# Rope scores as two packed fp32r products, and moved cast orders, in a two-layer conformer/attention trunk

## The chip, the cores and the metric

One core of one Trainium2 chip runs the whole program. The metric is the device time of one execution in microseconds, as the median of several runs.

## The reference

Two layers on 256 tokens of width 1024, all in float32. Each layer is half an FFN, a mixer, half an FFN; a last RMS norm closes the trunk. Layer 0 mixes by a convolution module, layer 1 by latent attention with 8 heads. What the change touches is the FFN and the attention scores:

```python
def swiglu_ffn(h, w1, w3, w2):
    return (jax.nn.silu(h @ w1) * (h @ w3)) @ w2      # 1024 -> 2816 -> 1024

for blk in range(seq // Q_BLOCK):                     # two query blocks of 128
    q0, q1 = blk * Q_BLOCK, (blk + 1) * Q_BLOCK
    s = (jnp.einsum("bqhd,bkhd->bhqk", q_nope[:, q0:q1], k_nope[:, :q1])
         + jnp.einsum("bqhr,bkr->bhqk", q_rope[:, q0:q1], k_rope[:, :q1])) * scale
    s = jnp.where(mask, s, -jnp.inf)                  # chunks of 64 tokens, causal
    p = jax.nn.softmax(s, axis=-1)
    outs.append(jnp.einsum("bhqk,bkhd->bqhd", p, v[:, :q1]))
```

The first query block sees 128 keys and the second 256. The nope part has 128 dimensions per head, the rope part 64, and the rope key is shared by all heads.

## The kernel before

**Products.** A float32 product is mostly done as three products in fp32r, a format with a shorter mantissa: each operand is split into a high part (a cast) and a low part (the value minus its high part), and `mm3` adds low times high, high times high and high times low. Its three matmuls are L332, L335 and L336. Weights come from memory in blocks of 128x2048 floats (`raw`); ScalarE (ACT) casts a block to `hi` in two pieces of 1024 columns and VectorE (DVE) subtracts to get `lo` (`load`, L246 and L247; `load_seven`, L214 and L200). SyncE (SP) issues all these transfers from one queue. Four raw buffers and five hi/lo buffers rotate, so a block is fetched as soon as an older one has been cast.

**FFN.** The 2816 columns go in chunks: five of 512 (c = 0 to 4) and one of 256 (c = 5). In FFNs 1, 2 and 3 (the second of layer 0 and both of layer 1) chunk 3 is done by seven block products in place of eight (`seven_products`): DVE first adds and subtracts blocks of the weights (L200, `raw<-raw,raw`), and between the products DVE adds finished parts to others (`u<-u,p`, line L258 by way of the helper `urgent`). After a chunk, ACT applies silu, DVE multiplies by the other half (`s<-s,u`) and turns 32x32 blocks (L478), two transfers through memory finish the transpose (`gd`, then `gb`, or `rows` for chunks 0 and 1), and ACT and DVE split the result into `Gh` and `Gl` (both L853). Such a pair of split instructions is a gate cast here, and they are listed in `gates`, two per chunk (NT is 2, one per block of 128 tokens).

**Attention.** KN and QN hold the nope keys and queries by head as float32; KR and QR hold the rope ones, also as float32. Heads are paired: rope rows of even heads stand in partitions 0 to 63 and of odd heads in 64 to 127, and the other half of the 128 rows is zero but for two rows that carry the mask (-1e30 times 1). `scores(hd)` runs for each query block one float32 product of KN and QN (L1584) and one of KR and QR (L1585) into one bank; `softmax` follows on DVE and ACT; `probs` transposes the probabilities on TensorE (PE) and ACT copies them (L1612); `values` multiplies with VV (L1621, L1622), and `evicted` splits the result into `Oh` (ACT, L1616) and `Ol` (DVE, L1617). The output projection runs between the heads, on blocks of two heads (`o<-lo,Oh` and so on). Three heads are scored ahead of the second half of the query projection (`nope`), the others after it.

**Order.** The order on each engine is fixed when the program is built: a list scheduler places instructions by priority (`urgent` lifts it), and `order(a, b)` forces a behind b. In `seven_products` such calls hold the gate casts of the chunk just before, and in `mla_in` a loop holds the casts of the first two output blocks behind certain steps of the softmax.

Of the kernel before, what the change touches and what calls it, by code (L numbers as in the profile page):

```python
# [11 lines left out]
F32 = mybir.dt.float32  # L12
# [7 lines left out]
P = 128  # L20
# [69 lines left out]
def trunk(ctx: ExitStack, tc: tile.TileContext, x, xt, first, pos, invf, gfin, wdw,  # L90
# [14 lines left out]
    def uid(s):  # L105
        n_uid[0] += 1
        return f"{s}_{n_uid[0]}"
# [54 lines left out]


    casts = {}

    turns = []
    last_read = [None]
# [21 lines left out]
    def load_seven(j, four, b, pieces):  # L189
        hi = wp.tile([P, HB], F32R, tag="hi", name=uid("hi"))  # L190
        lo = wp.tile([P, HB], F32R, tag="lo", name=uid("lo"))
        n = len(loaded)
        if j == 0:
            b[11], b[12] = fetched(four[0]), fetched(four[1])
        elif j == 1:
            b[22] = fetched(four[3])
        elif j == 2:
            b[21] = fetched(four[2])
        def sub(out, left, right):
            ins = nc.vector.tensor_sub(out, left, right)  # L200
            behind(ins)
            return ins

        if j == 1:
            sub(b[11], b[12], b[11])
            sub(b[12], b[22], b[12])
        elif j == 2:
            sub(b[11], b[22], b[11])
        elif j == 6:
            sub(b[11], b[21], b[11])  # L210
        raw = b[(11, 11, 11, 21, 12, 22, 11)[j]]
        for i in range(pieces):
            c = slice(i * HB // pieces, (i + 1) * HB // pieces)
            casts[n, i] = nc.scalar.copy(hi[:, c], raw[:, c]), sub(lo[:, c], raw[:, c], hi[:, c].bitcast(F32))  # L214
            behind(casts[n, i][0])
        return hi, lo
# [151 lines left out]
    def seven_products(xh, xl, forms, banks, late={}):  # L368


        def rows(a, tb):
            k = slice(4 * a, 4 * a + 4)
            return xh[:, k, tbs(tb)], xl[:, k, tbs(tb)]

        def product(a, b, fresh):
            load_ahead(W_BUFS - 1)
            (hi, lo), = weights(1, False)
            for k in range(4):
                c = slice(k * 512, k * 512 + 512)
                before[:] = [mm3(b, a[0][:, k], a[1][:, k], hi[:, c], lo[:, c], fresh and k == 0, k == 3, before, True)]  # L380

        n0 = n_used[0]
        before = []
        c11, c21, c12, c22 = banks[0, 0], banks[1, 0], banks[0, 1], banks[1, 1]
        product(rows(0, 0), c11, True)
        first = urgent(nc.scalar.copy)(c21, c11)
        for cast in late.values():
            order(cast, first.ins)
        product(forms[0], c22, True)
        kept = tmp.tile([P, 512], F32, tag="s", name=uid("p5"))  # L390
        last = urgent(nc.scalar.copy)(kept, c22)
        product(forms[1], c21, False)
        add = urgent(nc.vector.tensor_add)(c12, c21, kept)
        order(casts[n0 + 5, 0][1], add.ins)
        for high, low in gates[-NT:] if not late else ():
            order(high, last.ins)
            order(low, add.ins)
        low_gates = [low for high, low in gates[-NT:] if not late]
        product(rows(1, 0), c11, False)
        product(forms[2], c21, False)  # L400
        add = urgent(nc.vector.tensor_add)(c22, c21, kept)
        order(casts[n0 + 6, 0][1], add.ins)
        for low in low_gates[1:]:
            order(low, casts[n0 + 6, PIECES - 1][1].ins)
        product(forms[3], c12, False)
        product(rows(1, 1), c21, False)
# [8 lines left out]
    def tbs(tb):  # L415
        return slice(tb * P, (tb + 1) * P)
# [986 lines left out]
    def rope(pool, dst, src, n, cc, sn, tb, after=()):  # L1403

        w = n * 64
        t1, t2 = (pool.tile([P, w], F32, tag=f"rp{w}", name=uid("rp"), bufs=3 if n > 1 else 4) for _ in range(2))
        a = t1[:, :w].rearrange("p (n i f) -> p n i f", i=2, f=32)
        b = t2[:, :w].rearrange("p (n i f) -> p n i f", i=2, f=32)
        full = [P, n, 2, 32]
        turned = [nc.vector.tensor_tensor(a, src, cc[:, tb, :, :].unsqueeze(1).to_broadcast(full), op=ALU.mult)]  # L1410
        for i in range(2):
            turned.append(nc.vector.tensor_tensor(b[:, :, i, :], src[:, :, 1 - i, :],
                                                  sn[:, tb, i, :].unsqueeze(1).to_broadcast([P, n, 32]), op=ALU.mult))
        for ins in turned:
            for first in after:
                order(ins, first.ins)
        nc.vector.tensor_add(dst, t1[:, :w], t2[:, :w])
# [6 lines left out]
    def mla_in(act, X, make_next, cc, sn):  # L1424
# [4 lines left out]
        CKl = act.tile([P, 2, S], F32R, tag="CKl", name="CKl")  # L1429


        KR = act.tile([P, 2, S], F32, tag="KR", name="KR")
        QR = act.tile([P, 2, H // 2, S], F32, tag="QR", name="QR")
        for x, fill in ((KR, -1e30), (QR, 1.0)):
            nc.gpsimd.memset(x, 0.0)
            for parity in range(2):
                for tb in range(NT):
                    row = 64 * (1 - parity) + 32 * tb
                    t = tb * P + (CHUNK if x is KR else 0)
                    nc.gpsimd.memset(x[row:row + 1, parity, ..., t:t + CHUNK], fill)  # L1440

        last_low = [None]

# [108 lines left out]
        last = nope(part, QN, 4, CQh, CQl, 512, 0, (0, 4), turned)  # L1552
        for t in range(NT):
            b = transposed(kd[t], 0, 1, (last,))
            for i in range(2):
                half = slice(64 * i, 64 * i + 64)
                nc.scalar.copy(KR[half, i, tbs(t)], b[half, :P])
        for tb in range(NT):
            b = transposed(qr[tb], 0, 4, (last,)).rearrange("p (j t) -> p j t", t=P)
            for parity, copy in ((0, nc.scalar.copy), (1, nc.vector.tensor_copy)):  # L1560
                half = slice(64 * parity, 64 * parity + 64)
                urgent(copy)(QR[half, parity, :, tbs(tb)], b[half])
        kpart, = weights()
        nope(kpart, KN, 2, CKh, CKl, D, 0, (0, H))
        (hi, lo), = weights()
        for tb in range(NT):
            for d in range(2):
                b = bank("A", "v")
                for k in range(2):
                    c = slice(k * D + d * 512, k * D + d * 512 + 512)  # L1570
                    mm3(b, CKh[:, k, tbs(tb)], CKl[:, k, tbs(tb)], hi[:, c], lo[:, c], k == 0, k == 1)
                kept = nc.scalar.copy(VV[:, tb, d * 512:(d + 1) * 512], b)

        Oh = act.tile([P, H, S], F32R, tag="Oh", name="Oh")
        Ol = act.tile([P, H, S], F32R, tag="CQ", name="Ol")

        score_last, maxima, powers, scaled = [], [], [], []

        def scores(hd):
            b = bank("B", "sc")  # L1580
            sc = {0: b[:, :P], 1: b[:, P:P + S]}
            for qb in range(NT):
                n = (qb + 1) * P
                nc.tensor.matmul(sc[qb], QN[:, hd, tbs(qb)], KN[:, hd, :n], start=True, stop=False)  # L1584
                last = nc.tensor.matmul(sc[qb], QR[:, hd % 2, hd // 2, tbs(qb)], KR[:, hd % 2, :n], start=False,  # L1585
                                        stop=True)
            score_last.append(last)
            return softmax(sc)

# [19 lines left out]
        def probs(pr):  # L1609
            b = transposed(pr, 0, 3)  # L1610
            pt = act.tile([P, 3 * P], F32, tag="ptT", name=uid("ptT"), bufs=2)
            nc.scalar.copy(pt, b[:, :3 * P])  # L1612
            return pt

        def evicted(hd, b):
# [3 lines left out]
        def values(hd, pt):  # L1619
            b = bank("C", "pv")  # L1620
            nc.tensor.matmul(b[:, :S], VV[:, 0, hd * VH:(hd + 1) * VH], pt[:, :S], start=True, stop=False)  # L1621
            nc.tensor.matmul(b[:, P:S], VV[:, 1, hd * VH:(hd + 1) * VH], pt[:, S:], start=False, stop=True)  # L1622

            (urgent if hd in (3, 4, 5, 6) else lambda f: f)(evicted)(hd, b)

        pr, pt = {}, {}
        part, = weights(1, False)
# [1 line left out]

        table = urgent(nc.scalar.activation)(small.tile([P, 1], F32, tag="silu", name="exp"), neghalf, AF.Exp)  # L1630
        order(table, kept.ins)
        pr[0] = scores(0)
        pr[1] = scores(1)
        pr[2] = scores(2)

        for j, i, highs, lows in ((0, 0, None, maxima[2]), (0, 1, None, scaled[0]), (1, 0, powers[2], scaled[1]),
                                  (1, 1, powers[2], scaled[2])):
            for cast, first in zip(casts[n_used[0] + j, i], (highs, lows)):
                if first is not None:
                    order(cast, first.ins)  # L1640
        nope(part, QN, 4, CQh, CQl, 512, 4, (0, 4), score_last[-1:])
        o = Rows(Oh, Ol, H)
        for i in range(2, H + 3):
# [5 lines left out]
                load_ahead(i - 1 + (i == 4))  # L1649
            if i - 2 < H:  # L1650
                pt[i - 2] = probs(pr[i - 2])
            if i - 3 in pt:
                values(i - 3, pt[i - 3])
            if i in (6, 8):
# [164 lines left out]
```

## Time and profile before

| | |
|---|---|
| time, median of 3 runs | 897.49 us (896.9 to 898.99) |
| the profiled execution | 896.07 us, its span 894.3 us |
| PE busy | 886.9 us, 99% of the span |
| DVE busy | 743.1 us (83%) |
| ACT busy | 571.8 us (64%) |
| transfers | 198.94 MB, mean 222 GB/s |
| granted TensorE clock | 0.999 |

The span is what the profile sees from the first to the last instruction; 1.8 us lie around it. A record of a matmul has a modelled end, so its length is more than the time until the next one may start; the time that a matmul costs is read from the starts of those that follow each other. A float32 matmul leaves two records, one in fp32r leaves one.

### The profile page before, as it was taken

How to read it: one execution, taken by the hardware profiler on the slowest of the kernel's cores; microseconds unless marked ns; L12 is line 12 of the kernel's file. 1: busy time of each engine (PE TensorE's matmuls, PEld its weight loads, DVE VectorE, ACT ScalarE, POOL GpSimd, SP SyncE). 2: the span in 40 equal slices, each digit the busy share in tenths (PEclk: the TensorE clock that was granted, in tenths of full speed). 3: DMA queues.
4: the chain of work that ended last, by engine and by line, in shares of the span. 5: the costliest groups of instructions: out<-in, count | busy, mean ns of one | idle time of the engine just before them, and what ended most of it. 6: DMA issues, size and time to landing. Idle time of an engine off the chain costs nothing.

```text
span 894.3 us, 12241 instructions
## 1 busy us (share of the span) xinstructions
PE 886.9 (99%) x4221; PEld 745.9 (83%) x4221; DVE 743.1 (83%) x1083; ACT 571.8 (64%) x993; POOL 104.2 (12%) x227
## 2 busy tenths in 40 slices
PE   9999999999999999999999999999999999999997
PEld 7888888898988888888888888888899888888886
DVE  6787789579998999999588989995768579989973
ACT  7966458488886646667375566673677566474752
POOL 1000000069962000000010000001400010000000
PEclk9999999999999999999999999999999999999999
DMA  9987629834215864939759369495635349378541
GB/s 330 375 303 274 232 59 355 295 121 172 106 60 194 289 258 144 374 109 388 259 175 339 118 218 357 123 392 182 223 142 189 141 154 342 104 260 317 180 196 48
DMA packets 71055, 198.94 MB, mean 222 GB/s; under 512 B 12369, under 2 KB 41937, under 8 KB 51665
## 3 DMA queue, kind: packets, MB, share of 16 engines
q1 hardware_dynamic: 70560, 197.47, 61.8%
q8 instruction: 33, 0.54, 0.2%
q10 hardware_dynamic: 432, 0.69, 0.2%
q14 instruction: 30, 0.24, 0.1%
HBM read 181.87 MB, written 16.25 MB: 222 GB/s over the span
## 4 chain that ended last, share of the span: by engine, by line
PE 92%; DVE 4%; ACT 2%; DMA 1%; issue 0%; SPq 0%; POOL 0%; DVEq 0%; ACTq 0%
PE u L336 16%; PE u L335 16%; PE u L332 16%; PE o L335 9%; PE o L336 9%; PE o L332 9%; PE gate L1005 2%; PE u L411 2%; DVE acc L1094 2%; PE u L1005 2%; PE tp L446 1%; PE a L335 1%; PE a L332 1%; PE a L336 1%; PE nope L336 1%; PE nope L332 1%
## 5 line engine op out<-in xcount | busy, mean ns | idle before, releaser
L247 DVE TENSOR_TENSOR lo<-raw,hi 128x1024 fp32r<-128x1024 f32 (+1 forms) x236 | 276.2, 1212 | 38.8 <-ACT hi L246 37.6
L246 ACT CAST hi<-raw 128x1024 fp32r<-128x1024 f32 (+1 forms) x238 | 236.8, 1044 | 89.3 <-DMA raw<-in_f2w 30.8
L332 PE MATMUL u<-lo,Xh 128*128 128x512 f32 x612 | 238.4, 389 | 0.1
L336 PE MATMUL u<-hi,Xl 128*128 128x512 f32 x612 | 238.3, 389 | 0.0
L335 PE MATMUL u<-hi,Xh 128*128 128x512 f32 x612 | 238.1, 389 | 0.0
L332 PEld LDWEIGHTS u<-lo,Xh 128*128 128x128 f32 x612 | 114.9, 188 | 24.5 <-ACT Xh L598 0.5
L336 PEld LDWEIGHTS u<-hi,Xl 128*128 128x128 f32 x612 | 114.9, 188 | 24.3 <-DVE Xl L465 0.5
L335 PEld LDWEIGHTS u<-hi,Xh 128*128 128x128 f32 x612 | 114.9, 188 | 23.8
L214 ACT CAST hi<-raw 128x1024 fp32r<-128x1024 f32 x98 | 97.7, 1050 | 51.8 <-DVE raw L200 44.9
L200 DVE TENSOR_TENSOR lo<-raw,hi 128x1024 fp32r<-128x1024 f32 x98 | 115.6, 1216 | 7.1 <-ACT hi L214 7.1
L332 PE MATMUL o<-lo,Gh 128*128 128x512 f32 (+1 forms) x276 | 106.6, 386 | 0.0
L335 PE MATMUL o<-hi,Gh 128*128 128x512 f32 (+1 forms) x276 | 106.5, 386 | 0.0
L336 PE MATMUL o<-hi,Gl 128*128 128x512 f32 (+1 forms) x276 | 106.5, 386 | 0.0
L437 POOL TENSOR_TENSOR ms<-ss 128x1 f32<-128x1 f32 x16 | 8.1, 510 | 597.6 <-ACT junk L429 597.6
L200 DVE TENSOR_TENSOR raw<-raw,raw 128x2048 f32<-128x2048 f32 x28 | 63.9, 2283 | 1.8 <-DMA raw<-in_f2w 0.9
L332 PEld LDWEIGHTS o<-lo,Gh 128*128 128x128 f32 x276 | 51.8, 188 | 10.5
L335 PEld LDWEIGHTS o<-hi,Gh 128*128 128x128 f32 x276 | 51.9, 188 | 10.5
L336 PEld LDWEIGHTS o<-hi,Gl 128*128 128x128 f32 x276 | 51.8, 188 | 10.4
L1094 DVE SCALAR_TENSOR_TENSOR acc<-V,dw,acc 128x128 f32<-128x128 f32 (+1 forms) x174 | 53.9, 391 | 0.0
L1115 ACT ACTIVATE prod<-V,dw 128x128 f32<-128x128 f32 (+1 forms) x128 | 45.6, 415 | 1.8 <-POOL Y L1116 1.0
L956 ACT ACTIVATE s<-u,R 128x512 f32<-128x512 f32 (+1 forms) x48 | 30.9, 647 | 24.8 <-PE u L336 24.1
L797 DVE SCALAR_TENSOR_TENSOR h<-o,rh,h 128x512 f32<-128x512 f32 (+1 forms) x18 | 12.9, 719 | 29.2 <-PE o L336 29.2
(265 smaller groups left out, 1257.7 us busy)
## 6 DMA issues: line engine op xcount, KB each, us to landing
raw<-in_f2w SPq DMA_DIRECT2D x66, 1024.0 KB, 6.2
raw<-in_f1w SPq DMA_DIRECT2D x62, 1024.0 KB, 6.5
raw<-in_cw SPq DMA_DIRECT2D x12, 1024.0 KB, 5.5
gd<-gt SPq DMA_DIRECT2D x160, 64.0 KB, 3.0
gb<-gd SPq DMA_DIRECT2D x24, 256.0 KB, 2.8
rows<-gd SPq DMA_DIRECT2D x16, 256.0 KB, 4.4
raw<-in_wo SPq DMA_DIRECT2D x4, 1024.0 KB, 4.9
hd<-rows SPq DMA_DIRECT2D x56, 64.0 KB, 2.4
```

The costliest lines, as they stand in the source:

```text
L200: ins = nc.vector.tensor_sub(out, left, right)
L214: casts[n, i] = nc.scalar.copy(hi[:, c], raw[:, c]), sub(lo[:, c], raw[:, c], hi[:, c].bitcast(F32))
L246: casts[len(loaded), i] = (nc.scalar.copy(hi[:, c], raw[:, c]), low.tensor_sub(lo[:, c], raw[:, c], hi[:, c].bitcast(F32)))
L247: low.tensor_sub(lo[:, c], raw[:, c], hi[:, c].bitcast(F32)))
L332: mm = nc.tensor.matmul(o, ah, bl, start=start, stop=False, skip_group_check=seeded)
L335: nc.tensor.matmul(o, ah, bh, start=False, stop=False, skip_group_check=seeded)
L336: return nc.tensor.matmul(o, al, bh, start=False, stop=stop, skip_group_check=seeded)
L411: mm = nc.tensor.matmul(o, al if kind == "x" else ah, bl if kind == "l" else bh, start=start and n == 0, stop=stop and n == len(kinds) - 1)
L956: nc.scalar.activation(s[:, :w], u[0, tb][:, :w], AF.Silu, scale=X.r[tb])
L1005: mm = nc.tensor.matmul(u[:, t], w[:, c], X.x[:, k, t], start=(k == 0), stop=(k == KT - 1))
L1094: dve_last.append(nc.vector.scalar_tensor_tensor(out if j == j1 - 1 else y, v, w, y, op0=ALU.mult, op1=ALU.add))
L1115: prods_last.append(nc.scalar.activation(p, v, AF.Copy, scale=w))
```

## The change

Three parts.

1. The rope part of the scores. The rope keys are split into a high part KA, held in both halves of the rows, and a low part in KR; the rope queries into a high part in QR and, in a new tile QA, the low part in the half that QR leaves to zeros and the mask, with a copy of the high part in the other half. Then QA times KA gives high times high plus low times high in one product of 128 rows, and QR times KR gives high times low and the mask in another. Both are fp32r. So a query block takes one float32 and two fp32r matmuls in place of two float32 ones. The splits change the copies: two ACT copies for KA and four DVE subtractions for KR in place of four ACT copies; four ACT copies of QR, four DVE subtractions and four DVE copies for QA in place of two ACT and two DVE copies. The second transpose of the queries stands ahead of more of the value products than before.
2. The casts of the first two output blocks: the high ones of the second block now wait for the copies of the first two transposed probabilities, not for the third head's exponentials; the first block's high casts are held by nothing, as before. `evicted` of head 2 is lifted too.
3. In `seven_products`, the low gate casts of the chunk before the last are held behind the third weight difference (`thirds`), and those of the last chunk are held behind casts of the products' last two weight blocks (the high ones) and behind the low cast of the very last (the low ones).

```diff
@@ load_seven
         elif j == 2:
-            sub(b[11], b[22], b[11])
+            thirds[n] = sub(b[11], b[22], b[11])
@@ seven_products
-        last = urgent(nc.scalar.copy)(kept, c22)
+        urgent(nc.scalar.copy)(kept, c22)
...
-        for high, low in gates[-NT:] if not late else ():
-            order(high, last.ins)
-            order(low, add.ins)
-        low_gates = [low for high, low in gates[-NT:] if not late]
+        for high, low in gates[-2 * NT:-NT] if not late else ():
+            order(low, thirds[n0 + 2].ins)
+        late_gates = gates[-NT:] if not late else ()
...
-        for low in low_gates[1:]:
+        for n, (high, low) in enumerate(late_gates):
+            order(high, casts[n0 + 5 + n, PIECES - 1][0].ins)
             order(low, casts[n0 + 6, PIECES - 1][1].ins)
@@ rope
-        ... bufs=3 if n > 1 else 4) for _ in range(2))
+        ... bufs=6 if n > 1 else 4) for _ in range(2))
@@ mla_in
         for t in range(NT):
             b = transposed(kd[t], 0, 1, (last,))
+            nc.scalar.copy(KA[:, tbs(t)], b[:, :P])
             for i in range(2):
                 half = slice(64 * i, 64 * i + 64)
-                nc.scalar.copy(KR[half, i, tbs(t)], b[half, :P])
+                nc.vector.tensor_sub(KR[half, i, tbs(t)], b[half, :P], KA[half, tbs(t)].bitcast(F32))
...
-            for parity, copy in ((0, nc.scalar.copy), (1, nc.vector.tensor_copy)):
-                half = slice(64 * parity, 64 * parity + 64)
-                urgent(copy)(QR[half, parity, :, tbs(tb)], b[half])
+            for parity in range(2):
+                half, rest = (slice(64 * i, 64 * i + 64) for i in (parity, 1 - parity))
+                high = QR[half, parity, :, tbs(tb)]
+                turned_last = urgent(nc.scalar.copy)(high, b[half])
+                both = act.tile([P, 512], F32R, tag="rp512", ...)
+                urgent(nc.vector.tensor_sub)(both[rest], b[half], high.bitcast(F32))
+                urgent(nc.vector.tensor_copy)(both[half], high)
+                QA[parity, tb] = both
@@ scores
-                nc.tensor.matmul(sc[qb], QN[:, hd, tbs(qb)], KN[:, hd, :n], start=True, stop=False)
-                last = nc.tensor.matmul(sc[qb], QR[:, hd % 2, hd // 2, tbs(qb)], KR[:, hd % 2, :n], start=False,
-                                        stop=True)
+                three = [(QN[:, hd, tbs(qb)], KN[:, hd, :n]), (QA[hd % 2, qb][:, hd // 2], KA[:, :n]),
+                         (QR[:, hd % 2, hd // 2, tbs(qb)], KR[:, hd % 2, :n])]
+                for i, (rows_of, keys) in enumerate(three if qb == 0 else three[1:] + three[:1]):
+                    mm = nc.tensor.matmul(sc[qb], rows_of, keys, start=i == 0, stop=i == 2)
...
+            if i < 4:
+                order(late[i - 2], copies[-1].ins)
```

The scheduler turns this into a new order. The first place is DVE in chunk 3 of FFN 1, from the two additions between products (`u<-u,p`) to the first weight block of chunk 4 (`lo_3473`; `Gl` is the low gate cast of the two token blocks). Before:

```order
L258 TENSOR_TENSOR u_3393<-u_3391,p_553_3431 128x512
L853 TENSOR_TENSOR Gl_2854<-gb_3372,Gh_2853 128x4x128
L200 TENSOR_TENSOR lo_3434<-raw_3295,hi_3433 128x1024
L200 TENSOR_TENSOR raw_3235<-raw_3305,raw_3235 128x2048
L200 TENSOR_TENSOR lo_3434<-raw_3295,hi_3433 128x1024
L258 TENSOR_TENSOR u_3392<-u_3391,p_553_3431 128x512
L200 TENSOR_TENSOR lo_3453<-raw_3235,hi_3452 128x1024 x2
L853 TENSOR_TENSOR Gl_2854<-gb_3386,Gh_2853 128x4x128
L247 TENSOR_TENSOR lo_3473<-raw_3471,hi_3472 128x1024
L258 TENSOR_TENSOR s_3532<-s_3532,u_3393 128x512
L247 TENSOR_TENSOR lo_3473<-raw_3471,hi_3472 128x1024
```

And now, on the same engine at the same place (line numbers are one higher):

```order
L201 TENSOR_TENSOR lo_3434<-raw_3295,hi_3433 128x1024
L259 TENSOR_TENSOR u_3393<-u_3391,p_553_3431 128x512
L201 TENSOR_TENSOR lo_3434<-raw_3295,hi_3433 128x1024
L201 TENSOR_TENSOR raw_3235<-raw_3305,raw_3235 128x2048
L259 TENSOR_TENSOR u_3392<-u_3391,p_553_3431 128x512
L201 TENSOR_TENSOR lo_3453<-raw_3235,hi_3452 128x1024 x2
L854 TENSOR_TENSOR Gl_2854<-gb_3372,Gh_2853 128x4x128
L854 TENSOR_TENSOR Gl_2854<-gb_3386,Gh_2853 128x4x128
L259 TENSOR_TENSOR s_3532<-s_3532,u_3393 128x512
L248 TENSOR_TENSOR lo_3473<-raw_3471,hi_3472 128x1024 x2
```

One cast of `lo_3434` moved ahead of the first addition; both gate casts and the product `s<-s,u` now stand between `lo_3453` and the first piece of `lo_3473`, where one gate cast stood. The same rows move in FFNs 2 and 3.

The second place is PE at the scores of head 5 (`sc_6425` before, `sc_6450` now), with what surrounds them. Before:

```order
L336 MATMUL o_6347<-hi_6138,Ol 128x512
L1584 MATMUL sc_6425<-KN,QN 128x128
L1585 MATMUL sc_6425<-KR,QR 128x128
L1584 MATMUL sc_6425<-KN,QN 128x256
L1585 MATMUL sc_6425<-KR,QR 128x256
L446 MATMUL tp_6441<-ident,pr_6362 128x128 x3
```

And now:

```order
L336 MATMUL o_6369<-hi_6153,Oh 128x512
L1602 MATMUL sc_6450<-KN,QN 128x128
L1602 MATMUL sc_6450<-KA,QA_6136 128x128
L1602 MATMUL sc_6450<-KR,QR 128x128
L1602 MATMUL sc_6450<-KA,QA_6149 128x256
L1602 MATMUL sc_6450<-KR,QR 128x256
L1602 MATMUL sc_6450<-KN,QN 128x256
L1640 MATMUL pv_6445<-ptT_6398,VV 128x256
```

Four matmuls became six, and the group stands ahead of head 1's values (`pv_6445`), no longer behind them.

The third place is ACT from the exponentials of head 4 (`pr_6389` before, `pr_6414` now) to head 1's `Oh`. Before:

```order
L1600 ACTIVATE pr_6389,sm_6388<-sc_6382,nm_6387 128x128
L1600 ACTIVATE pr_6389,sm_6388<-sc_6382,nm_6387 128x256
L246 COPY hi_6399<-raw_6398 128x1024 x2
L246 COPY hi_6407<-raw_6406 128x1024 x2
L1616 COPY Oh<-pv_6420 128x256
```

And now:

```order
L1619 ACTIVATE pr_6414,sm_6413<-sc_6405,nm_6412 128x128
L1619 ACTIVATE pr_6414,sm_6413<-sc_6405,nm_6412 128x256
L247 COPY hi_6424<-raw_6423 128x1024 x2
L247 COPY hi_6432<-raw_6431 128x1024 x2
L1635 COPY Oh<-pv_6445 128x256
```

Nothing moved here: the four weight casts still stand between the exponentials and head 1's `Oh`.

More of the change, by code (lines that the diff above doesn't have):

```diff
@@ L164, in trunk @@
     casts = {}
+    thirds = {}
     turns = []
@@ L1405, in rope @@
         w = n * 64
-        t1, t2 = (pool.tile([P, w], F32, tag=f"rp{w}", name=uid("rp"), bufs=3 if n > 1 else 4) for _ in range(2))
+        t1, t2 = (pool.tile([P, w], F32, tag=f"rp{w}", name=uid("rp"), bufs=6 if n > 1 else 4) for _ in range(2))
         a = t1[:, :w].rearrange("p (n i f) -> p n i f", i=2, f=32)
@@ L1429, in mla_in @@
         CKl = act.tile([P, 2, S], F32R, tag="CKl", name="CKl")
-        KR = act.tile([P, 2, S], F32, tag="KR", name="KR")
-        QR = act.tile([P, 2, H // 2, S], F32, tag="QR", name="QR")
+        KA = act.tile([P, S], F32R, tag="KA", name="KA")
+        QA = {}
+        KR = act.tile([P, 2, S], F32R, tag="KR", name="KR")
+        QR = act.tile([P, 2, H // 2, S], F32R, tag="QR", name="QR")
         for x, fill in ((KR, -1e30), (QR, 1.0)):
-            nc.gpsimd.memset(x, 0.0)
+            nc.gpsimd.memset(x.bitcast(F32), 0.0)
             for parity in range(2):
@@ L1439, in mla_in @@
                     t = tb * P + (CHUNK if x is KR else 0)
-                    nc.gpsimd.memset(x[row:row + 1, parity, ..., t:t + CHUNK], fill)
+                    nc.gpsimd.memset(x[row:row + 1, parity, ..., t:t + CHUNK].bitcast(F32), fill)
         last_low = [None]
@@ L1554, in mla_in @@
             b = transposed(kd[t], 0, 1, (last,))
+            nc.scalar.copy(KA[:, tbs(t)], b[:, :P])
             for i in range(2):
                 half = slice(64 * i, 64 * i + 64)
-                nc.scalar.copy(KR[half, i, tbs(t)], b[half, :P])
+                nc.vector.tensor_sub(KR[half, i, tbs(t)], b[half, :P], KA[half, tbs(t)].bitcast(F32))
+        turns_of = [], []
         for tb in range(NT):
-            b = transposed(qr[tb], 0, 4, (last,)).rearrange("p (j t) -> p j t", t=P)
-            for parity, copy in ((0, nc.scalar.copy), (1, nc.vector.tensor_copy)):
-                half = slice(64 * parity, 64 * parity + 64)
-                urgent(copy)(QR[half, parity, :, tbs(tb)], b[half])
+            b = transposed(qr[tb], 0, 4, (last,), turns_of[tb]).rearrange("p (j t) -> p j t", t=P)
+            for parity in range(2):
+                half, rest = (slice(64 * i, 64 * i + 64) for i in (parity, 1 - parity))
+                high = QR[half, parity, :, tbs(tb)]
+                turned_last = urgent(nc.scalar.copy)(high, b[half])
+                both = act.tile([P, 512], F32R, tag="rp512", name=uid("QA"), bufs=6).rearrange("p (j t) -> p j t", t=P)
+                urgent(nc.vector.tensor_sub)(both[rest], b[half], high.bitcast(F32))
+                urgent(nc.vector.tensor_copy)(both[half], high)
+                QA[parity, tb] = both
         kpart, = weights()
@@ L1570, in mla_in @@
                     c = slice(k * D + d * 512, k * D + d * 512 + 512)
-                    mm3(b, CKh[:, k, tbs(tb)], CKl[:, k, tbs(tb)], hi[:, c], lo[:, c], k == 0, k == 1)
+                    mm3(b, CKh[:, k, tbs(tb)], CKl[:, k, tbs(tb)], hi[:, c], lo[:, c], k == 0, k == 1,
+                        turns_of[0][-1:] if (tb, d) == (0, 0) else turns_of[1][-1:])
                 kept = nc.scalar.copy(VV[:, tb, d * 512:(d + 1) * 512], b)
@@ L1575, in mla_in @@
         Ol = act.tile([P, H, S], F32R, tag="CQ", name="Ol")
-        score_last, maxima, powers, scaled = [], [], [], []
+        score_last, maxima, powers, scaled, copies, late = [], [], [], [], [], []
         def scores(hd):
@@ L1581, in scores @@
             sc = {0: b[:, :P], 1: b[:, P:P + S]}
+            last = None
             for qb in range(NT):
                 n = (qb + 1) * P
-                nc.tensor.matmul(sc[qb], QN[:, hd, tbs(qb)], KN[:, hd, :n], start=True, stop=False)
-                last = nc.tensor.matmul(sc[qb], QR[:, hd % 2, hd // 2, tbs(qb)], KR[:, hd % 2, :n], start=False,
-                                        stop=True)
+                three = [(QN[:, hd, tbs(qb)], KN[:, hd, :n]), (QA[hd % 2, qb][:, hd // 2], KA[:, :n]),
+                         (QR[:, hd % 2, hd // 2, tbs(qb)], KR[:, hd % 2, :n])]
+                for i, (rows_of, keys) in enumerate(three if qb == 0 else three[1:] + three[:1]):
+                    mm = nc.tensor.matmul(sc[qb], rows_of, keys, start=i == 0, stop=i == 2)
+                    if last is not None:
+                        order(mm, last.ins)
+                    last = mm
             score_last.append(last)
@@ L1611, in probs @@
             pt = act.tile([P, 3 * P], F32, tag="ptT", name=uid("ptT"), bufs=2)
-            nc.scalar.copy(pt, b[:, :3 * P])
+            copies.append(nc.scalar.copy(pt, b[:, :3 * P]))
             return pt
@@ L1622, in values @@
             nc.tensor.matmul(b[:, P:S], VV[:, 1, hd * VH:(hd + 1) * VH], pt[:, S:], start=False, stop=True)
-            (urgent if hd in (3, 4, 5, 6) else lambda f: f)(evicted)(hd, b)
+            (urgent if hd in (2, 3, 4, 5, 6) else lambda f: f)(evicted)(hd, b)
         pr, pt = {}, {}
@@ L1631, in mla_in @@
         order(table, kept.ins)
+        order(table, turned_last.ins)
         pr[0] = scores(0)
@@ L1634, in mla_in @@
         pr[2] = scores(2)
[L1636 to L1640, printed above, removed]
+        for j, i, lows in ((0, 0, maxima[2]), (0, 1, scaled[0]), (1, 0, scaled[1]), (1, 1, scaled[2])):
+            high, low = casts[n_used[0] + j, i]
+            order(low, lows.ins)
+            if j == 1:
+                late.append(high)
         nope(part, QN, 4, CQh, CQl, 512, 4, (0, 4), score_last[-1:])
```

## The prediction

> **What bounds the kernel now.** I read the page first: busy times, then the chain that ended last.
>
> ```profile
> PE 886.9 (99%) x4221; PEld 745.9 (83%) x4221; DVE 743.1 (83%) x1083; ACT 571.8 (64%) x993; POOL 104.2 (12%) x227
> PE 92%; DVE 4%; ACT 2%; DMA 1%; issue 0%; SPq 0%; POOL 0%; DVEq 0%; ACTq 0%
> ```
>
> PE is busy for 886.9 us, 99% of the span, and makes 92% of the chain. There is next to no idle time on it, and all its waits together, in the view of waits, are two:
>
> ```profile
> PE warm L324 <- DVE still L319: 1.0, 1, 1.0
> PE u L411 <- ACT Xh L640: 0.2, 1, 0.2
> ```
>
> So the sum is simple to set up: a matmul that goes away or becomes shorter gives its cost, one to one, and a weight that arrives later than PE wants it takes its lateness, one to one. Nothing else counts. I therefore look for two things: what the new scores cost on PE, and which moved casts now end behind PE's wish.
>
> **The scores on PE.** The chain in the first heads' stretch gives costs from start to start:
>
> ```profile
> 676.06 0.12 PE nope L336
> ...
> 676.51 0.22 PE sc L1584 x2
> 676.73 0.22 PE sc L1585 x2
> 676.96 0.43 PE sc L1584 x2
> 677.39 0.43 PE sc L1585 x2
> ```
>
> A float32 product costs 0.22 at 128 columns and 0.43 at 256. `nope` is fp32r with 256 columns: 0.12. For the second query block one float32 product of 0.43 becomes two fp32r ones of 0.12: a gain of 0.43 − 0.24 = 0.19 per head, 8 heads, 1.5 us. For the first block one product of 0.22 becomes two fp32r products of 128 columns, and the trace has no such product. Its bounds: the line through the nearest fp32r rows, 0.12 at 256 and 0.23 at 512 columns (two starts below, 354.00 − 353.77), gives 0.065 at 128; that a product keeps a floor is seen in the one-column products, where ten records against two differ by (1.17 − 0.29) / 8 = 0.11 each; the far end is the float32 cost, 0.22.
>
> ```profile
> 246.12 1.17 PE L1132 MATMUL ms<-ones,sq 128*128 128x1 f32 x10
> 247.46 0.29 PE L1132 MATMUL ms<-ones,sq 128*128 128x1 f32 x2
> ```
>
> I take the floor, 0.11: fewer columns than 256 save little, as 256 stand at 0.12 already. Two products then cost 0.22, as much as the one they replace: no gain, no loss. The ends: 8 x (0.22 − 0.13) = 0.7 us gained, or 8 x 0.22 = 1.8 lost.
>
> On this price a rule of the Trainium skill speaks, in "TensorE: Matmul & The Clock Gate", section "Back-to-back issue gap": in a stream of weight loads and matmuls, one with 128 columns takes about 81 ns. By it the two would cost an estimated 0.16 and the eight heads would gain 0.46 us more; the trace's floor of 0.11 speaks against it, though that is of float32 records, and no row here is an fp32r product of 128 columns.
>
> **Head 1's output.** The scores come 7 times before the output projection's first product with head 1's `Oh`:
>
> ```profile
> 681.35 0.37 ACT L1600 ACTIVATE pr<-sc,nm 128x128 f32<-128x128 f32 x1 [0.33 <-DVE nm L1598]
> 682.15 3.88 ACT L246 CAST hi<-raw 128x1024 fp32r<-128x1024 f32 x4
> 685.93 0.38 ACT L1616 CAST Oh<-pv 128x256 fp32r<-128x256 f32 x1
> ```
>
> ```profile
> 686.20 0.59 PE L1585 MATMUL sc<-KR,QR 128*128 128x256 f32 x2
> 686.44 0.58 PE L332 MATMUL o<-lo,Oh 128*128 128x512 f32 x1
> ```
>
> That cast is not lifted and stays behind four weight casts on ACT. It ends at 686.31, the product stands at 686.44: 0.13 to spare. PE will be there 7 x 0.19 = 1.33 earlier. If ACT did not move at all PE would wait 1.33 − 0.13 = 1.2; if it moved as far, nothing. ACT can follow only by its idle time ahead of the four casts, and just ahead of them that is 0.33, behind DVE's `nm`: about 1.2 − 0.33 = 0.9. The second record of the scores at 686.20 runs for a part of the product's record, which makes it a little less. I take 0.8, between 0 and 1.2. The lift of head 2's `evicted` does not touch this one. The attention then gives −1.5 + 0.8 = −0.7 us.
>
> **The gate casts.** This is the place in FFN 1:
>
> ```profile
> 348.83 0.70 DVE L258 TENSOR_TENSOR u<-u,p 128x512 f32<-128x512 f32 x1 [1.53 <-PE u L336]
> ...
> 354.51 0.69 DVE L258 TENSOR_TENSOR u<-u,p 128x512 f32<-128x512 f32 x1
> 355.11 2.35 DVE L200 TENSOR_TENSOR lo<-raw,hi 128x1024 fp32r<-128x1024 f32 x2
> 357.38 0.69 DVE L853 TENSOR_TENSOR Gl<-gb,Gh 128x512 fp32r<-128x512 f32 x1
> 357.98 1.22 DVE L247 TENSOR_TENSOR lo<-raw,hi 128x1024 fp32r<-128x1024 f32 x1
> 359.12 0.68 DVE L258 TENSOR_TENSOR s<-s,u 128x512 f32<-128x512 f32 x1
> 359.71 3.49 DVE L247 TENSOR_TENSOR lo<-raw,hi 128x1024 fp32r<-128x1024 f32 x3
> ```
>
> ```profile
> 353.77 0.39 PE L336 MATMUL u<-hi,Gl 128*128 128x512 f32 x1
> 354.00 0.39 PE L332 MATMUL u<-lo,Gh 128*128 128x512 f32 x1
> 359.44 0.40 PE L332 MATMUL u<-lo,Xh 128*128 128x512 f32 x1
> ```
>
> Chunk 4's first low piece (L247 at 357.98) ends at 359.20, and PE's first product with it starts at 359.44. DVE runs without a gap from 354.51. In the new order the second `Gl` (0.60 from start to start, 357.38 to 357.98) and `s<-s,u` (0.59, 359.12 to 359.71) come ahead of that piece as well. Against this, the first `Gl` no longer stands ahead of the second addition, which can start earlier: not before its product's last matmul is done, 353.77 + 0.39 = 354.16, so by 0.35 at most. The piece ends at 359.20 + 0.60 + 0.59 − 0.35 = 360.04, which is 0.60 after PE wants it; without the 0.35, 0.95 after. I take 0.7. The piece of `lo` that moved ahead of the first addition costs nothing: it lies in DVE's idle 1.53 there, and without that cover it would put the addition back by its own 1.22. The order is the same in FFNs 2 and 3, and so is the margin, 533.60 − (532.14 + 1.22) = 0.24 and 798.16 − (796.70 + 1.22) = 0.24:
>
> ```profile
> 532.14 1.22 DVE L247 TENSOR_TENSOR lo<-raw,hi 128x1024 fp32r<-128x1024 f32 x1
> 796.70 1.22 DVE L247 TENSOR_TENSOR lo<-raw,hi 128x1024 fp32r<-128x1024 f32 x1
> ```
>
> ```profile
> 533.60 0.40 PE L332 MATMUL u<-lo,Xh 128*128 128x512 f32 x1
> 798.16 0.40 PE L332 MATMUL u<-lo,Xh 128*128 128x512 f32 x1
> ```
>
> Three stalls of 0.7 make +2.1 us, between 3 x 0.6 = 1.8 and 3 x 0.95 = 2.9. The high gate casts go behind weight casts on ACT, which puts weights earlier there. ACT frees raw buffers no later for it, so SP's queue of transfers is not moved: the next block's casts wait for their transfer already, not for ACT.
>
> ```profile
> 358.27 2.00 ACT L246 CAST hi<-raw 128x1024 fp32r<-128x1024 f32 x2 [0.88 <-DMA raw<-in_f2w]
> ```
>
> **The splits of the rope rows.** DVE gets four subtractions and two more copies for QA, and four small subtractions for KR. The old copy of this shape took 0.69, and a subtraction that writes fp32r with as many columns the same 0.69 (`Gl` above). Six of them and four KR ones of at most 0.35 make 4.1 + 1.4 = 5.5 us.
>
> ```profile
> 661.25 0.69 DVE L258 COPY QR<-tp 64x512 f32<-64x512 f32 x1 [1.90 <-ACT QR L258]
> 665.80 0.69 DVE L258 COPY QR<-tp 64x512 f32<-64x512 f32 x1 [3.86 <-ACT QR L258]
> 668.73 0.62 DVE L1597 TENSOR_REDUCE nm<-sc 128x1 f32<-128x128 f32 x2 [2.23 <-PE sc L1585]
> ```
>
> DVE's idle time in this stretch is 1.90 + 3.86 + 2.23 = 8.0, so they are hidden. If the cover were gone, the first scores would wait by what is over, and DVE's `nm` behind them. ACT gets two more copies of this size, 1.4 at most; the DVE idle of 1.90 and 3.86 above, spent waiting for ACT's QR copies, shows how far apart those come, and both engines' splits are needed by the scores alone. The second edit puts the second output block's high casts from 672.38 behind the second copy of probabilities:
>
> ```profile
> 672.38 2.02 ACT L246 CAST hi<-raw 128x1024 fp32r<-128x1024 f32 x2
> 678.19 0.48 ACT L1612 COPY ptT<-tp 128x384 f32<-128x384 f32 x1 [1.00 <-PE tp L446]
> ```
>
> ```profile
> 692.09 0.47 PE L332 MATMUL o<-lo,Oh 128*128 128x512 f32 x1
> ```
>
> That copy ends at 678.67, two casts of 1.0 and two low ones of 1.2 make it 683.1 at the latest if nothing comes between, and the block is first multiplied at 692.09: 9 us to spare, so I give it nothing.
>
> **Sum.** −0.7 + 2.1 = +1.4 us on the profiled execution: 896.07 becomes 897.5. The median shown, 897.49, is 1.42 above that execution; the same step on it gives 898.9. A measurement of this kernel can tell about 0.2%, 1.8 us, from no change.
>
> **Rivals.**
>
> 1. *The 128-column fp32r products cost as much as float32 ones, 0.22.* Then the scores give −1.5 + 1.8 = +0.3, PE reaches head 1's output no earlier, and that wait falls away. With the FFN's 2.1 this is +2.4, 899.9: slower by more than 0.2%. For: no fp32r row of 128 columns shows a lower price, and none shows what a switch between the formats costs. Against: fp32r at 256 columns is nearly twice as fast as float32. It decides from about 0.19 per product, where 8 x (0.38 − 0.22) = 1.3 of the 1.5 is given back.
> 2. *The gate casts stay hidden*, because PE comes to chunk 4 a little later in the new order or DVE has spare time earlier. Then only the attention counts: −0.7, 896.8, no change. Against: DVE's row at 357.38 to 363 has no idle time, and the margin is 0.24 in all three.
> 3. *The rope's splits come late.* Each QA tile hangs on a chain: transpose, ACT copy, DVE subtraction, DVE copy. At 1.2 each for the six, 7.2 + 1.4 = 8.6 are more than the 8.0 idle, and PE would wait at the first scores, at most by the last tile's whole chain, 0.7 + 2 x 1.2 = 3.1: with the +1.4 it is +4.5, 902.0. Against: the old copies of this shape take 0.69, and above 1.1 each the idle time is used up, not before.
> 4. *No stall and cheap 128-column products*: −1.5 − 0.7 = −2.2, 895.3, faster. It takes both the line's 0.065 and head 1's cast in time.
>
> **How the numbers follow.** The forecast, +1.4, has a chance of 0.50; its own range is 898.2 to 899.8 (stalls of 1.8 to 2.9, wait of 0 to 1.2). Rival 1 has 0.31, rival 2 0.09, rival 3 0.05, rival 4 0.05. Time 898.9. The range of 896.7 to 900.9 holds the forecast, rival 1 with the dearer stalls (+2.9 + 0.3 = +3.2, 900.7) and rival 2; rivals 3 and 4 lie outside. Slower by over 1.8 us: rival 1, rival 3 and the part of the forecast above 899.3, about 0.3 of its 0.50: 0.51. Faster by over 1.8: rival 4, 0.05. The rest, 0.44, is no change.
>
> **What would show it.** In the changed trace: two fp32r products of 128 columns from start to start in about 0.22, those of 256 in 0.24; a wait of PE of some 0.8 at the first `o<-lo,Oh` of head 1, behind ACT; three waits of PE of 0.6 to 0.95 at the first `u<-lo,Xh` of chunk 4, behind DVE's `lo`, with both `Gl` and `s<-s,u` ahead of it; no wait at the first scores. I am wrong if PE has no wait in the FFNs, or if the scores of a head cost more than the 1.3 us of today.

## The result, and the profile after

The changed kernel takes 898.62 us (median of 14 runs, 897.15 to 899.75); in the same rounds the kernel before took 896.96 (14 runs, 895.65 to 898.99). The ratio is 1.0014, with a 95% interval of 1.0008 to 1.0021: 0.7 to 1.9 us slower, in the middle 1.3. The forecast was +1.4. Against the 0.2% that the prediction took as what can be told this is no change; against zero it is a small loss.

The page of the changed kernel's profile, span and busy times:

```profile
span 897.0 us, 12269 instructions
PE 886.6 (99%) x4221; PEld 743.6 (83%) x4221; DVE 748.1 (83%) x1093; ACT 571.0 (64%) x993; POOL 105.1 (12%) x227
```

PE's busy time is the same to 0.3 us, though its work became shorter; the records of matmuls overlap, so this row cannot show a gain of 1.5 us. The view of PE's waits can show the losses (engine, line, whom it waited for: total us, times, longest):

```profile
PE u L333 <- DVE lo L248: 1.8, 3, 0.6
PE warm L325 <- DVE still L320: 1.0, 1, 1.0
PE o L333 <- ACT Oh L1635: 0.7, 1, 0.7
PE rb L1152 <- POOL rc L1148: 0.4, 1, 0.4
PE u L412 <- ACT Xh L641: 0.2, 1, 0.2
```

Rows 1 and 3 are the two waits that the prediction named, in their places and at their sizes: three of 0.6 at chunk 4, and 0.7 at head 1's `Oh`. The fourth, a wait for POOL in the convolution module, was not expected; the experiments come back to it.

This is FFN 1 on DVE, from the second addition to chunk 4's first low pieces, and PE's product behind it (start, length, and in brackets the idle time ahead and its releaser):

```profile
354.63 0.70 DVE L259 TENSOR_TENSOR u<-u,p 128x512 f32<-128x512 f32 x1 [0.49 <-PE u L337]
355.26 2.36 DVE L201 TENSOR_TENSOR lo<-raw,hi 128x1024 fp32r<-128x1024 f32 x2
357.54 1.29 DVE L854 TENSOR_TENSOR Gl<-gb,Gh 128x512 fp32r<-128x512 f32 x2
358.74 0.68 DVE L259 TENSOR_TENSOR s<-s,u 128x512 f32<-128x512 f32 x1
359.34 2.35 DVE L248 TENSOR_TENSOR lo<-raw,hi 128x1024 fp32r<-128x1024 f32 x2
```

```profile
359.64 0.39 PE L337 MATMUL u<-hi,Xl 128*128 128x512 f32 x1
360.61 0.50 PE L333 MATMUL u<-lo,Xh 128*128 128x512 f32 x1 [0.58 <-DVE lo L248]
360.95 0.39 PE L336 MATMUL u<-hi,Xh 128*128 128x512 f32 x1
```

Both `Gl` and `s<-s,u` stand ahead of the first `lo`, and PE waits 0.58 for it. The stall costs more than that. The wait is counted from the modelled end of the product before; from start to start that product and the wait take 0.97 (359.64 to 360.61), where such a product takes 0.23 in a full stream, so 0.74 is lost. And the product that starts after the wait keeps PE for 0.34 (360.61 to 360.95), 0.11 more than in the stream.

And this is the attention: the chain at head 3's scores (start, us, what), and PE at head 1's `Oh`:

```profile
678.08 0.33 PE tp L447 x3
678.41 1.13 PE sc L1602 x8
```

```profile
687.39 0.59 PE L1602 MATMUL sc<-KN,QN 128*128 128x256 f32 x2
688.70 0.50 PE L333 MATMUL o<-lo,Oh 128*128 128x512 f32 x1 [0.72 <-ACT Oh L1635]
```

By the chain a head's scores take 1.13 on PE in place of the 1.30 of before; by the starts of PE's own records, from the first of head 3's scores to the transposition behind them, 1.12 in place of 1.31, a gain of 0.19. The wait behind ACT, listed as 0.72, takes a large part of the 1.5 back.

Put one beside the other, the starts of the same products in the two traces show where the 2.7 us between the two spans arise. From the last product before the stall in chunk 4 to the second one behind it the changed kernel falls back by 0.85 (FFN 1), 0.86 (FFN 2) and 0.85 (FFN 3), together 2.6; over the attention, from 650 to 715 us, it gains 0.7; the other 0.7 to 0.8 lies in layer 0 and at the start of FFNs, in steps of 0.1 to 0.7, some of them gains. The experiments below are read by the same comparison of starts with the trace of before.

### The profile page after: what moved, and what is told of

Read it like the earlier page. It is cut to its first block, busy times and chain, and to the rows that moved or that the text cites. A ratio compares the mean times of both kernels' runs of the same rounds, so it can differ in the third digit from the quotient of the medians.

```text
span 897.0 us, 12269 instructions
## 1 busy us (share of the span) xinstructions
PE 886.6 (99%) x4221; PEld 743.6 (83%) x4221; DVE 748.1 (83%) x1093; ACT 571.0 (64%) x993; POOL 105.1 (12%) x227
## 4 chain that ended last, share of the span: by engine, by line
PE 93%; DVE 3%; DMA 2%; ACT 1%; issue 0%; SPq 0%; POOL 0%; ACTq 0%; DVEq 0%
PE u L333 16%; PE u L337 16%; PE u L336 16%; PE o L337 9%; PE o L333 9%; PE o L336 9%; PE u L1006 3%; PE gate L1006 3%; PE u L412 2%; PE o L1242 1%; PE pairs L1049 1%; PE tp L447 1%; DMA hd<-rows 1%; PE a L336 1%; PE a L333 1%; PE a L337 1%
```

## The experiments

The expectations speak of Theory A (the prediction's account: the gate casts cost, the scores gain and lose a part to head 1's `Oh`) and of rivals, each told in its place. Times are medians beside those of the kernel before from the same rounds: 897.0 for the first four, 896.8 for the last two.

**1. The third edit taken back.** The changed kernel with the old gate casts:

```diff
-        for high, low in gates[-2 * NT:-NT] if not late else ():
-            order(low, thirds[n0 + 2].ins)
...
+        for high, low in gates[-NT:] if not late else ():
+            order(high, last.ins)
+            order(low, add.ins)
```

> The changed kernel with the third edit taken back: the gate casts stand as before. Theory A (three FFN stalls cost about 2.4 us, the attention gains 1.5 and loses 0.7 by the wait for head 1's Oh): 0.7 us less than before, 896.3 where before has 897.0; no wait of PE at chunk 4's first u<-lo,Xh, still one of about 0.7 at o<-lo,Oh. Rival B (the new scores themselves are the cost, and the FFN stalls only move time that is lost later anyway): 0.5 to 1.5 us more than before. Rival C (the 0.7 us that the changed kernel's trace is late in layer 0 outside the FFN's chunk 4, of which 0.4 is a wait for POOL's rc, belongs to the change): the same +0.7 stands in layer 0 and the time equals before.

896.22, ratio 0.999 (0.998 to 1.0): 0.8 less than before by the medians. PE's waits, all of them:

```profile
PE warm L325 <- DVE still L320: 1.0, 1, 1.0
PE o L333 <- ACT Oh L1635: 0.7, 1, 0.7
PE rb L1152 <- POOL rc L1148: 0.4, 1, 0.4
```

The three stalls are gone and the one at `Oh` stays, as Theory A has it; B wanted a slower kernel, which the interval excludes. Over the attention this trace gains 0.6. C is half tested: the wait for `rc` stands here too, yet the time is not higher.

**2. The third edit alone**, on the kernel before (the same lines the other way round).

> The kernel before with the third edit alone. Theory A: three waits of PE of about 0.6 us behind DVE's lo in chunk 4 of FFNs 1, 2 and 3, and 1.8 to 2.4 us more than before: 898.8 to 899.4. Rival B: the waits are there, but the time is within 0.5 us of before. Rival C: 2.5 to 3.1 more than before, with the same lateness in layer 0.

898.75, ratio 1.0018 (1.0008 to 1.0028): 1.8 more by the medians. PE's waits, then DVE and PE in FFN 1:

```profile
PE u L333 <- DVE lo L248: 1.8, 3, 0.6
PE warm L325 <- DVE still L320: 1.0, 1, 1.0
PE rb L1152 <- POOL rc L1148: 0.4, 1, 0.4
PE u L412 <- ACT Xh L641: 0.2, 1, 0.2
```

```profile
358.17 0.68 DVE L259 TENSOR_TENSOR s<-s,u 128x512 f32<-128x512 f32 x1
358.77 2.36 DVE L248 TENSOR_TENSOR lo<-raw,hi 128x1024 fp32r<-128x1024 f32 x2
```

```profile
360.04 0.50 PE L333 MATMUL u<-lo,Xh 128*128 128x512 f32 x1 [0.59 <-DVE lo L248]
```

Up to here this execution is 0.14 us ahead of the one of before, so its clock can be read against the prediction's working: the product's start at 360.04 is 360.18 on that clock, 0.74 later than the 359.44 of before, where the prediction had the piece end at 360.04. By the starts, each of the three stalls puts PE back by 0.85 here too. Experiments 1 and 2 add up to +1.0 by the medians, the whole change to +1.7, with intervals of about 0.9 us on either side of each experiment and 0.6 of the whole: A holds, B falls. C falls by the spread: the 0.4 for `rc` stands in this experiment, which has the old scores, and in experiment 1, which has the old gate casts, and it is absent in experiments 3, 4 and 6, which have the new scores. So it belongs to neither edit and is scatter between executions. The rest of the 0.7 to 0.8 outside the changed places was not traced to a cause, but it differs as freely: the changed kernel's 0.3 at the start of FFN 2, for one, is 0.1 to 0.6 in the experiments.

**3. Head 1's `Oh` ahead of two of the four weight casts**, on experiment 1:

```diff
-            nc.scalar.copy(Oh[:, hd, :], b[:, :S])
+            high = nc.scalar.copy(Oh[:, hd, :], b[:, :S])
+            if hd == 1:
+                for piece in range(PIECES):
+                    order(casts[n_used[0] + 3, piece][0], high.ins)
```

> scores_only with ACT's last two casts of output block 3 held behind head 1's Oh cast, so that this cast stands behind two weight casts and not four. Theory A: the wait at o<-lo,Oh (0.7) goes, and the time is 1.5 us less than before, 895.5, and 0.7 less than scores_only. Rival D (the wait of PE there hides another: the next thing late is Ol of head 1 on DVE, or the held weight casts are late for their own products): as scores_only, within 0.3 us, with a new wait in the attention that is as long.

895.15, ratio 0.9976 (0.9967 to 0.9985): 1.9 less than before, and 1.1 less than experiment 1. ACT in that place:

```profile
683.08 1.99 ACT L247 CAST hi<-raw 128x1024 fp32r<-128x1024 f32 x2
684.96 0.37 ACT L1635 CAST Oh<-pv 128x256 fp32r<-128x256 f32 x1
685.22 2.01 ACT L247 CAST hi<-raw 128x1024 fp32r<-128x1024 f32 x2
```

And PE's first product with head 1's `Oh`:

```profile
686.21 0.58 PE L333 MATMUL o<-lo,Oh 128*128 128x512 f32 x1
```

Between 640 and 760 us PE now has no wait in the list, so no other wait stood behind that one, and rival D falls. The attention gains 1.7 by the starts, where experiment 1 gained 0.6: the wait listed as 0.7 cost about 1.1, which is also what the medians moved. (The two profiled spans are both 893.6; this execution has a wait of 0.6 at 11 us, in the first FFN, that the other has not.) This version beats both kernels: the scores' gain of 1.5 arrives once nothing is late behind it.

**4. The price of an fp32r product of 128 columns**, on experiment 3. The four products added to each head add nothing to the result:

```diff
+                for _ in range(4 if qb == 0 else 0):
+                    mm = nc.tensor.matmul(sc[0], *three[1], start=True, stop=True)
...
```

> scores_oh1 with four more KA,QA products of 128 columns ahead of each head's first query block, each begun afresh so that they add nothing: 32 more fp32r products of 128 columns, to price one. By the floor of 0.11: 3.5 us more than scores_oh1. By the line through 256 and 512 columns, 0.065: 2.1 more. By the float32 cost of 0.22: 7.0 more. By the 81 ns that the Trainium skill states (TensorE: Matmul & The Clock Gate, Back-to-back issue gap), 2.6 more. The cadence from start to start in the trace gives the price without the noise of the total.

900.01, ratio to before 1.0039 (1.0023 to 1.0054): 4.9 more than experiment 3 by the medians; between the two profiled spans, 897.2 and 893.6, it is 3.6. The weight loads give the cadence without that scatter (start, length of the group):

```profile
677.41 0.52 PEld L1602 LDWEIGHTS sc<-KA,QA 128*128 128x128 f32 x4
677.85 0.30 PEld L1607 LDWEIGHTS sc<-KN,QN 128*128 128x128 f32 x2
678.07 0.19 PEld L1607 LDWEIGHTS sc<-KA,QA 128*128 128x128 f32 x1
678.18 0.19 PEld L1607 LDWEIGHTS sc<-KR,QR 128*128 128x128 f32 x1
```

Four loads from 677.41 to 677.85: 0.11 each, and 0.11 again from 678.07 to 678.18. That is the prediction's floor, and 32 x 0.11 = 3.5 is what the spans show. By the starts, the attention alone accounts for it: 1.7 gained in experiment 3, 1.9 lost here, together 3.6. Neither the line's 0.065 nor the float32 price of 0.22 fits. The Trainium skill's "TensorE: Matmul & The Clock Gate" (Back-to-back issue gap) states about 81 ns for a matmul of 128 columns in a stream of weight loads and matmuls; for fp32r products that each have a weight load of their own this trace speaks against it, with 0.11. Why the medians give 4.9 rather than 3.6 stays open.

**5. One low gate cast given back**, on the changed kernel:

```diff
-            order(low, casts[n0 + 6, PIECES - 1][1].ins)
+            if n == 1:
+                order(low, casts[n0 + 6, PIECES - 1][1].ins)
```

> The changed kernel, but of the two low gate casts of chunk 3's group only the second stays behind the last weight block's low cast; the first is no longer held. The high casts' new place and the third weight difference's rule stay. Theory A (the stall is DVE's extra 0.60 for that one Gl ahead of chunk 4's first low piece, and PE wants the piece 0.6 before it ends): the three waits fall from 0.6 to 0.1 at most, and the time goes from 898.6 to about 896.8 or a little below. Rival E (the stall comes of the high gate casts' new place on ACT, or of s<-s,u ahead of the piece): three waits of 0.5 or more stay, and the time is within 0.5 us of the changed kernel.

897.34, ratio to before 1.0004 (0.9995 to 1.0013). PE's waits, then DVE in FFN 1:

```profile
PE warm L325 <- DVE still L320: 1.0, 1, 1.0
PE o L333 <- ACT Oh L1636: 0.7, 1, 0.7
PE rb L1153 <- POOL rc L1149: 0.4, 1, 0.4
PE o L337 <- DVE rows L365: 0.3, 1, 0.3
PE o L333 <- ACT o L259: 0.2, 1, 0.2
```

```profile
353.66 0.68 DVE L855 TENSOR_TENSOR Gl<-gb,Gh 128x512 fp32r<-128x512 f32 x1
354.26 0.69 DVE L259 TENSOR_TENSOR u<-u,p 128x512 f32<-128x512 f32 x1
354.86 2.36 DVE L201 TENSOR_TENSOR lo<-raw,hi 128x1024 fp32r<-128x1024 f32 x2
357.14 0.69 DVE L855 TENSOR_TENSOR Gl<-gb,Gh 128x512 fp32r<-128x512 f32 x1
357.74 0.68 DVE L259 TENSOR_TENSOR s<-s,u 128x512 f32<-128x512 f32 x1
358.34 2.36 DVE L248 TENSOR_TENSOR lo<-raw,hi 128x1024 fp32r<-128x1024 f32 x2
```

And PE at the piece:

```profile
359.24 0.39 PE L337 MATMUL u<-hi,Xl 128*128 128x512 f32 x1
359.61 0.50 PE L333 MATMUL u<-lo,Xh 128*128 128x512 f32 x1
359.94 0.40 PE L336 MATMUL u<-hi,Xh 128*128 128x512 f32 x1
```

One `Gl` is back in the gap ahead of the second addition, and the three waits are gone from the list, though `s<-s,u` and the other `Gl` still stand ahead of the piece and the high casts kept their new place. So the 0.60 of one cast on DVE made most of the stall, and E falls. A rest stays that the list does not show: the two products take 0.37 and 0.33 to the next start in place of 0.23 each, and by the starts PE is put back by 0.25 in each of the three FFNs, where the changed kernel has 0.85; so the three FFNs give back 1.8 in this trace, as A had it. The median is 1.3 below the changed kernel's (1.1 when each is taken against the kernel before in its own rounds); two small waits at other products, 0.3 and 0.2, are new in this execution and were not followed up.

**6. The second edit taken back too**, on experiment 1: the second output block's high casts stand behind head 2's exponentials again, and head 2's `evicted` isn't lifted.

```diff
-            if i < 4:
-                order(late[i - 2], copies[-1].ins)
...
+                                  (1, 1, powers[2], scaled[2])):
```

> scores_only with the second edit taken back as well (the second output block's high casts behind head 2's exponentials, head 2's evicted not lifted): the new scores alone. The prediction gave the second edit nothing: the time would be that of scores_only, 896.2, with the same wait of 0.7 at head 1's Oh. Rival F (PE comes to head 0's values about 1 us earlier than before, and the copies of the transposed probabilities then stand behind those weight casts on ACT): a wait of PE of about 1.3 at pv<-ptT,VV, which takes the place of the one at Oh, and 0.4 us more than scores_only.

896.63, ratio to before 0.9998 (0.9989 to 1.0007). PE's wait, and ACT ahead of it:

```profile
677.64 0.70 PE L1640 MATMUL pv<-ptT,VV 128*128 128x256 f32 x2 [1.22 <-ACT ptT L1631]
```

```profile
674.72 2.00 ACT L247 CAST hi<-raw 128x1024 fp32r<-128x1024 f32 x2
676.60 0.60 ACT L1531 COPY QN<-nope 128x512 f32<-128x512 f32 x1
677.08 0.89 ACT L1631 COPY ptT<-tp 128x384 f32<-128x384 f32 x2
```

Rival F is right about the mechanism: the wait of 1.22 at head 0's values takes the place of the 0.7 at `Oh`. What it costs, 0.4 between the medians, is within what the runs scatter. By the starts, the attention gains nothing here (0.04), where experiment 1 gained 0.6: in these traces the second edit is worth 0.6, and without it the new scores bring nothing in this stretch. Its two parts were taken back together; that the casts are the part that counts is read from the rows on ACT and not shown by a run of its own.

## Why the prediction was right, point by point

- **PE sets the end.** Right: the time moved the way of each wait that came or went (experiments 1, 2, 3 and 5). "One to one" was a little low: a wait listed as 0.58 put PE back by 0.85, and one listed as 0.7 by about 1.1.
- **The scores.** Right: 1.12 per head in place of 1.31, the 0.19 less that was forecast. The 128-column products cost 0.11 each (experiment 4), so the first query block gained nothing and the second all of it. Rivals 1 and 4 both hung on this price and fall with it.
- **Head 1's output.** The listed wait is 0.7 where 0.8 was taken, and the casts ahead of it were the cause (experiment 3). The attention's −0.7 came out as 0.7 gained; in it two small misses cancel, a gain of 1.7 without the wait where 1.5 was forecast, and a wait that cost about 1.1.
- **The gate casts.** Right about what stands ahead of the piece, short in size: three stalls of 0.7 were taken, the product comes 0.75 late and the loss is 0.85 each, 2.6 in place of 2.1. DVE was free 0.49 before the second addition, which waited for PE, as the 0.35 had supposed. Rival 2 falls.
- **The low piece moved ahead of the first addition.** The cover was misjudged, without harm. That piece waits for ACT, and the addition comes later behind it:

```profile
348.98 1.23 DVE L201 TENSOR_TENSOR lo<-raw,hi 128x1024 fp32r<-128x1024 f32 x1 [1.25 <-ACT hi L215]
350.12 0.69 DVE L259 TENSOR_TENSOR u<-u,p 128x512 f32<-128x512 f32 x1
```

The addition starts 1.3 later than before (348.83), of which 0.4 is the lateness of this execution by then. No wait of PE stands behind it.

- **The splits of the rope rows.** Hidden, as forecast, and cheaper than the bound: DVE's copies take 0.42, its small subtractions 0.30.

```profile
661.65 1.20 DVE L1564 TENSOR_TENSOR KR<-tp,KA 64x128 fp32r<-64x128 f32 x4
663.76 0.68 DVE L259 TENSOR_TENSOR QA<-tp,QR 64x512 fp32r<-64x512 f32 x1 [0.90 <-ACT QR L259]
664.47 0.42 DVE L259 CAST QA<-QR 64x512 fp32r<-64x512 f32 x1
```

No wait of PE at the first scores: rival 3 falls.

- **The second edit at nothing.** This step failed. I asked only when the moved casts' own block is wanted, 9 us later. What counts is who stood behind them on ACT: the copies of the probabilities, which the shorter scores want earlier. Without the edit PE waits 1.2 there (experiment 6) and the attention gains nothing in place of 0.6. The sum took the full gain of the scores without asking what else they need in time; that the change brings the edit along made it come out, which was luck.
- **The sum, the range and the chances.** The parts that the traces show are +2.6 and −0.7, so +1.9, at the upper end of the interval; the forecast was +1.4. The time of 898.9 started from a median of 3 runs, 897.49; from the 896.96 of the 14 runs it would have been 898.4, on the other side of the measured 898.62. The forecast's own range of 898.2 to 899.8 is narrower than its bounds give: 1.8 − 1.5 = +0.3 and 2.9 − 1.5 + 1.2 = +2.6 make 897.8 to 900.1. And the larger chance, 0.51, lay on more than 1.8 us slower, most of it on rival 1; what came was the 0.44 of no change.

## What to carry to other kernels

When one engine is full, price a change in two lists: what becomes shorter on that engine, and which operand's margin is smaller than what now stands ahead of it. A margin of 0.24 us here met a cast of 0.60, and one of 0.13 met a gain of 1.3; both could be read from the trace of before. A gain on the full engine first eats the margins of everything queued in order behind other work; free those (one cast moved ahead of two others here) and the gain arrives. And ask of each moved cast not only when its own result is wanted but also whom it no longer holds up.

## What the runs showed of the hardware that was not expected

A fp32r product of 128 columns with its own weight load costs 0.11 us from load to load, nearly as much as one of 256 columns (0.12): halving the columns saves next to nothing there. And a wait of PE costs more than it lists: from start to start a listed wait of 0.58 took 0.74, and the first 512-column product behind it takes 0.34 to the next start where the stream has 0.23, so that PE fell back by 0.85. A stall can even be there with no wait listed: in experiment 5 PE lost 0.25 at the same place.
